# Where the large SBUF buffers of a split-float32 decoder block begin: multiples of 512 bytes, and still weights 192 bytes in

## The chip, the cores and the metric

The kernel runs on one core of a Trainium2 chip. The metric is the device time of one execution in microseconds (us). The engines are named as the profile names them: PE is TensorE's matrix multiplication, PEld its weight load, DVE is VectorE, ACT is ScalarE, POOL is GpSimd and SP is SyncE, which here issues nearly all transfers.

## The reference

One decoder layer on 256 tokens of width 1024, in float32: a normalised input goes through one wide projection into two attention branches (8 heads each) and two gates; the gated sum of both branches goes through an output projection and a normalised residual; then comes a feed-forward part with a squared ReLU. Cut to the matrix work, which is what the change touches:

```python
proj = rms_norm(x) @ w_in                       # 1024 -> q,k,v | c_q 384 | c_kv 256 + 32 | gates 2048
q = (rms_norm(c_q) @ w_uq); kv = (rms_norm(c_kv) @ w_ukv)
o_a = moba(q, k, v) @ w_branch_a                # causal softmax, 8 heads x 64
o_b = mla(q, kv) @ w_branch_b
merged = sigmoid(g_a) * o_a + sigmoid(g_b) * o_b
x = x + rms_norm(merged @ w_out)                # 1024 x 1024
x = x + rms_norm(square(relu(rms_norm(x) @ w_up)) @ w_down)   # 1024 -> 4096 -> 1024
```

## The kernel before

**Split products.** Every large factor is cut into a high and a low part (`hi`, `lo`), so that one product is three matmuls of float32r: hi by hi, hi by lo, lo by hi (`mm3`, L179 and L182). Each matmul instruction has a stationary operand, 128 columns that PEld loads into the array (512 bytes in each partition), and a moving operand of 256, 288, 384 or 512 columns that is streamed past it (1024 to 2048 bytes in each partition). In the trace the load of the next matmul's stationary operand runs while the present matmul streams.

**Which side the weights are on.** There are two kinds of product.

- `a_chunk` (L267 on), `mms` in `mix`, the first part of the up projection (`up_a`) and `product` for the down projection keep a token operand (`xt`, `mg`, `x1`, `m`) still and move the weights, 288 to 512 columns at a time.
- `b_tile` and `nope` keep the weights still and move 256 token columns: the gates (`g*`, 16 units of 24 matmuls, 384 in all, woven into attention and done after it), `uq` and `uk` (60), the branch projections `br0` to `br7` (192), and the up projection from the fifth row block on (14 pairs, 48 matmuls each, 672).

The down projection comes once for each of 16 pairs of row blocks. The pairs in `PLAIN` are 24 matmuls of 512 moving columns. Of these, pairs 0, 5 and 10 take the weights from `t_hi` and `t_lo`, 14 and 15 from `u_hi` and `u_lo`. The 11 others have seven products (21 matmuls): first three with weights from `b_hi` and `b_lo` (9 matmuls), then four from `t_hi` and `t_lo` (12). The order of PE is that of the code. From pair to pair PE alternates 48 matmuls of the up projection with 21 or 24 of the down projection.

**How weights come.** `unit` (first half) loads a raw weight block into one of 6 `raw` buffers, ACT copies it to a `whi` buffer (5), DVE writes the difference to `wlo` (5). `load` and `split` do the same in the second half with `raw_u`, `raw_d` and the pairs of buffers `u`, `t`, `b`. SP issues these transfers in the order of the code, and each waits there until the tiles that lay in its place before have been read for the last time.

**Where buffers begin.** Pools are stacks: the pools `keep`, then `att`, grow from the left, `late` and `wts` from the right; in the second half `mlp0` takes the place of `att` and `mlp1` that of `wts` and `late`. Within a pool, tiles lie in the order in which they are first made, with their sizes. In the program before, the begins are these, in bytes past a multiple of 512 in each partition (every block that a matmul reads inside a buffer lies a multiple of 512 further on, but for the 288-column blocks):

| buffers | bytes past a multiple of 512 |
|---|---|
| `xt_hi`, `xt_lo`, `x1_hi`, `x1_lo`, `t_hi`, `t_lo`, `raw_u`, `raw_d` | 320 |
| `raw`, `whi`, `wlo`, `ct`, `mg`, `u`, `b`, `m_hi`, `m_lo` | 480 |
| `o_hi`, `o_lo` | 384 |
| `kz0`, `kz1`, `qT0` / `qT1` | 128 / 320 |

The text calls *offset* the begin of the moving operand less the begin of the next stationary operand, in bytes, by the remainder over 512. Before, it is 320 - 480 = -160, that is 352, where `xt` or `x1` moves past `whi`, `wlo` or `u`; 160 where `whi` or `wlo` moves past `xt`; 352 where `t` moves past `m`; 0 where `b` or `u` moves past `m`, `whi` or `wlo` past `mg`, `t` past `x1`; and 416 (-96) where `o` moves past `whi` or `wlo`.

Of the kernel before, what the change touches and what calls it, by code (L numbers as in the profile page):

```python
# [10 lines left out]
F32 = mybir.dt.float32  # L11
F32R = mybir.dt.float32r
# [23 lines left out]
WARM_UP = 8  # L36
LAG = 2
QUOTA_A, QUOTA_B = 1900, 1900

PLAIN = (0, 5, 10, 14, 15)  # L40

# [92 lines left out]
def block_kernel(ctx: ExitStack, tc: tile.TileContext, x, xt, pos_col, g_post_in, weights, out):  # L134
    nc = tc.nc
    table, _ = _block_table()

    keep = ctx.enter_context(tc.tile_pool(name="keep", bufs=1))

    first_half, attention_part = ExitStack(), ExitStack()  # L140
    late, wts = (first_half.enter_context(tc.tile_pool(name=n, bufs=b, side="right"))
# [11 lines left out]
    def after(later, earlier):  # L153

        tc.add_manual_dep(later.ins, earlier.ins.name,
                          mybir.DependencyInfo(mybir.DependencyClass.NoSync, mybir.DependencyReason.DATA),
                          reason="order")
# [1 line left out]
    last_split = []  # L159


    def unit(key, hi=None, lo=None, behind=None):


        off, width = table[key]
        raw = wts.tile([P, UNIT], F32, name="raw", tag="raw", bufs=6)[:, :width]
        if hi is None:
            hi = wts.tile([P, UNIT], F32R, name="whi", tag="whi")[:, :width]
            lo = wts.tile([P, UNIT], F32R, name="wlo", tag="wlo")[:, :width]
        nc.sync.dma_start(raw, weights[off:off + P * width].rearrange("(p c) -> p c", c=width))  # L170
        ops = nc.scalar.activation(hi, raw, AF.Copy), nc.vector.tensor_tensor(lo, raw, hi, op=OP.subtract)  # L171
        for op, first in zip(ops, behind or ()):
            after(op, first)
        last_split[:] = ops
        return hi, lo

    def mm3(ps, a_hi, a_lo, b_hi, b_lo, first, last, a_lo_last=False):
# [22 lines left out]
    inv_freq = att.tile([P, 16], F32, name="inv_freq")  # L200
    for i in range(16):
        nc.gpsimd.memset(inv_freq[:, i:i + 1], INV_FREQ[i])
    mask = att.tile([P, 3 * P], F32, name="mask")
    nc.gpsimd.memset(mask, 0.0)
    for c in (0, 2):
        m = mask[:, c * P:(c + 1) * P]
        nc.gpsimd.affine_select(m, m, pattern=[[-1, P]], base=0, channel_multiplier=1,
                                compare_op=OP.is_ge, fill=NEG)


    stat = keep.tile([P, 128], F32, name="stat")
    used = [0]

    def stat_cols(n):
        used[0] += n
        return stat[:, used[0] - n:used[0]]
# [86 lines left out]
    ctx.enter_context(tc.manual_schedule(engines={nc.tensor.engine}))  # L303


    zeros = att.tile([P, 512], BF16, name="zeros")
    nc.vector.memset(zeros, 0.0)
    first = stat_cols(1)
    nc.scalar.activation(first, zeros[:, :1], AF.Copy)
# [30 lines left out]
    cN = att.tile([P, NT, NC], F32, name="cN", tag="t6")  # L340
    kr = att.tile([P, NT, DQ], F32, name="kr")
    nc.gpsimd.memset(kr, 0.0)
    ss_c = stat_cols(2 * NT)
    for i, n in enumerate((QLORA, KVLORA)):
        for t in range(NT):
# [103 lines left out]
    next(v_chunk)  # L449


    o_hi = att.tile([P, 2, H // 2, S], F32R, name="o_hi", tag="m2")
    o_lo = att.tile([P, 2, H // 2, S], F32R, name="o_lo", tag="m3")

# [2 lines left out]
    def attention(br, products, v_of, scale):  # L457


        ranges = ((0, P), (P, 3 * P))  # L460
        probs, pts = {}, {}

        def softmax(h, sp):
            sm = att.tile([P, 3 * P], F32, name="sm", tag="sm", bufs=3)
            st = att.tile([P, 6], F32, name="st", tag="st", bufs=4)
            pr = att.tile([P, 3 * P], F32, name="pr", tag="pr", bufs=4)
            for t, (a, b) in enumerate(ranges):
                nc.vector.tensor_tensor_reduce(sm[:, a:b], sp[t], mask[:, a:b], scale=-scale, scalar=3.0e38,
                                               op0=OP.add, op1=OP.min, accum_out=st[:, t:t + 1])
                last_exp[0] = nc.scalar.activation(pr[:, a:b], sm[:, a:b], AF.Exp, bias=st[:, t:t + 1], scale=-1.0,  # L470
                                     accum_out=st[:, 2 + t:3 + t])
            nc.vector.reciprocal(st[:, 4:6], st[:, 2:4])
            for t, (a, b) in enumerate(ranges):
                nc.vector.tensor_scalar(pr[:, a:b], pr[:, a:b], st[:, 4 + t:5 + t], None, op0=OP.mult)
            probs[h] = pr

        def turned(h):
            pp = wk_tile()
            transposes(pp, [probs[h][:, c * P:(c + 1) * P] for c in range(3)])
            pts[h] = att.tile([P, 3 * P], F32, name="pt", tag="pt", bufs=3)  # L480
            nc.scalar.copy(pts[h], pp[:, :3 * P])

        def values(hp):
            op = wk_tile()
            for j in range(2):
                h = 2 * hp + j
                o = op[j * 64:(j + 1) * 64]
                nc.tensor.matmul(o[:, 0:S], v_of(0, h), pts[h][:, 0:S], start=True, stop=False)  # L488
                nc.tensor.matmul(o[:, P:S], v_of(1, h), pts[h][:, S:S + P], start=False, stop=True)  # L489
            nc.scalar.copy(o_hi[:, br, hp], op[:, :S])  # L490
            nc.vector.tensor_tensor(o_lo[:, br, hp], op[:, :S], o_hi[:, br, hp], op=OP.subtract)

        def step(i):
            if i < H:
                for h, sp in products(i).items():
                    softmax(h, sp)
            if 0 <= i - LAG < H:
                turned(i - LAG)
            j = i - LAG - 2
            if j >= 0 and j % 2 == 0:  # L500
                values(j // 2)

        return [lambda i=i: step(i) for i in range(H + LAG + 1)]
# [31 lines left out]
    def gate_tiles():  # L535
        for m in range(KD):
            ps = acc_tile()
            for br in range(2):
                yield from b_tile(ps[:, br * S:(br + 1) * S], unit(f"g{m}_{br}"), xt_hi, xt_lo, KD)
            nc.vector.tensor_tensor(gate(m), ps.rearrange("p (b s) -> p b s", b=2),  # L540
                                    rstd_row[:, None, :].to_broadcast([P, 2, S]), op=OP.mult)
            gates_done[0] += 1
# [7 lines left out]
    def latent_work():  # L550
# [25 lines left out]
            nc.scalar.copy(dst[:, 1:4:2], psv[64:128])  # L576

        for i in range(2):
            yield from nope(unit(f"uq{i}_0"), 256, 0, range(3), qMT[0:NOPE, 4 * i:4 * i + 4])
        u = unit("uk0")  # L580
        for i in range(2):
            yield from nope(u, 512, i, (3, 4), kMT[0:NOPE, 4 * i:4 * i + 4])
        ps = [acc_tile() for _ in range(NT)]
# [34 lines left out]
    gates_up_to(1)  # L618
    left = KD - gates_done[0]
    for m in range(KD):  # L620
        u = unit(f"br{m}")
        ps = wk_tile()
        for br in range(2):
            run(b_tile(ps[:, br * S:(br + 1) * S], u, o_hi[:, br], o_lo[:, br], 4, base=4 * br))
            sig = nc.scalar.activation(gate(m)[:, br], gate(m)[:, br], AF.Sigmoid, bias=col(B_GATE, br * KD + m))
            after(sig, last_exp[0])
        pr = att.tile([P, 2 * S], F32, name="mp", tag="mp", bufs=2)
        nc.vector.tensor_tensor(pr, ps, gate(m).rearrange("p b s -> p (b s)"), op=OP.mult)
        sm = att.tile([P, S], F32, name="ms", tag=("ra", "rb")[m % 2])
        nc.vector.tensor_tensor(sm, pr[:, :S], pr[:, S:], op=OP.add)  # L630
        nc.scalar.copy(mg_hi[:, m], sm)
        nc.vector.tensor_tensor(mg_lo[:, m], sm, mg_hi[:, m], op=OP.subtract)
        gates_up_to(max(m + 2, KD - left + 1 + m))
# [10 lines left out]

        return mlp0 if tag in ("raw_u", "raw_d", "th", "tl", "m0n", "r") else mlp1[0]

    def split(src, tag, behind=(), parts=1):

        n = src.shape[-1]
        size = {"b": 3 * 512}.get(tag, PAIR)  # L650
        hi = mlp(f"{tag}h").tile([P, size], F32R, name=f"{tag}_hi", tag=f"{tag}h")[:, :n]
        lo = mlp(f"{tag}l").tile([P, size], F32R, name=f"{tag}_lo", tag=f"{tag}l")[:, :n]
        for i in range(parts):
            c = slice(i * n // parts, (i + 1) * n // parts)
            ops = nc.scalar.activation(hi[:, c], src[:, c], AF.Copy), \  # L655
                nc.vector.tensor_tensor(lo[:, c], src[:, c], hi[:, c], op=OP.subtract)  # L656
            if behind:
                for op, first in zip(ops, behind[i]):
                    after(op, first)
        return hi, lo  # L660
# [196 lines left out]
    for i in range(WARM // 2, n_pairs):  # L857
        ps = wk_tile()
        behind = {2: (turned[0, 1], turned[1, 0]), 3: (turned[1, 1],)}.get(i, ())
        w = split(load(f"up{2 * i}", "u"), "u", behind, max(len(behind), 1))  # L860
        for j in range(2):
            run(b_tile(ps[:, j * S:(j + 1) * S], w, x1_hi, x1_lo, KD, base=j * KD))
            if i == WARM // 2 and j == 0:
                for f0 in range(0, WARM, 2):
                    m0_ps = wk_tile()
                    transposes(m0_ps, [m0[:, t, k * P:(k + 1) * P] for k in (f0, f0 + 1) for t in (1, 0)])
                    square(f0 // 2, m0_ps, False)
        square(i, ps, True)
        if i >= BEHIND:
            down(i - BEHIND, (turned[1, 1],) if i == BEHIND else ())  # L870
# [69 lines left out]
```

## Time and profile before

| | us |
|---|---|
| median of 3 runs | 371.86 (371.44 to 371.88) |
| the profiled execution's own time | 371.55 |
| its span, first to last instruction | 369.8 |
| PE busy, share of the span | 359.7 (97%) |
| DVE busy | 298.0 (81%) |
| ACT busy | 248.8 (67%) |
| moved by transfers | 66.2 MB, mean 179 GB/s |

A matmul's recorded duration is modelled and overlaps that of the next one, so the duration of a single row is not its cost. The cost is the distance from one start to the next: a stretch of the trace divided by the number of matmuls that start in it. A count (x) in a stretch takes in the one or two matmuls that began before it and are still draining: one where the earlier ones are 384 or 512 columns wide, two where they have 256 or 288. [...]

### The profile page before, as it was taken

How to read it: one execution, taken by the hardware profiler on the slowest of the kernel's cores; microseconds unless marked ns; L12 is line 12 of the kernel's file. 1: busy time of each engine (PE TensorE's matmuls, PEld its weight loads, DVE VectorE, ACT ScalarE, POOL GpSimd, SP SyncE). 2: the span in 40 equal slices, each digit the busy share in tenths (PEclk: the TensorE clock that was granted, in tenths of full speed). 3: DMA queues.
4: the chain of work that ended last, by engine and by line, in shares of the span. 5: the costliest groups of instructions: out<-in, count | busy, mean ns of one | idle time of the engine just before them, and what ended most of it. 6: DMA issues, size and time to landing. Idle time of an engine off the chain costs nothing.

```text
span 369.8 us, 6081 instructions
## 1 busy us (share of the span) xinstructions
PE 359.7 (97%) x2319; PEld 321.5 (87%) x2319; DVE 298.0 (81%) x555; ACT 248.8 (67%) x375; POOL 6.5 (2%) x29
## 2 busy tenths in 40 slices
PE   8999999999999999999999999999999999999992
PEld 4699888989998999998879998889999888999881
DVE  4898898985766576796686999999989979978556
ACT  6889569996758755647289966767747766545422
POOL 6000000000000000000000000000000000000000
PEclk9999999999999999999999999999999999999997
DMA  7987763455434356574804756456564447330002
GB/s 252 403 327 244 258 205 106 125 218 152 136 96 133 113 172 178 179 268 179 334 3 165 268 194 252 180 193 228 228 217 161 170 177 284 131 115 0 2 0 113
DMA packets 15036, 66.20 MB, mean 179 GB/s; under 512 B 1696, under 2 KB 2208, under 8 KB 10912
## 3 DMA queue, kind: packets, MB, share of 16 engines
q1 hardware_dynamic: 14688, 65.30, 50.5%
q10 hardware_dynamic: 288, 0.52, 0.4%
q8 instruction: 18, 0.29, 0.3%
q14 instruction: 10, 0.08, 0.1%
q0 software_dynamic: 32, 0.00, 0.0%
HBM read 64.77 MB, written 1.05 MB: 178 GB/s over the span
## 4 chain that ended last, share of the span: by engine, by line
PE 91%; DVE 4%; DMA 2%; ACT 1%; SPq 1%; issue 1%; DVEq 0%; ACTq 0%
PE acc L182 30%; PE wk L182 27%; PE acc L179 15%; PE wk L179 13%; PE wk L368 3%; DMA raw<-in_weights 2%; PE wk L488 1%; PE wk L520 1%; ACT sq L242 1%; DVE y L898 1%; PE wk L489 1%; DVE x_lo L714 0%; PE wk L519 0%; SPq L255 0%; DVE y L685 0%
## 5 line engine op out<-in xcount | busy, mean ns | idle before, releaser
L171 DVE TENSOR_TENSOR wlo<-raw,whi 128x1024 fp32r<-128x1024 f32 (+4 forms) x58 | 65.7, 1139 | 20.3 <-ACT whi L171 20.3
L171 ACT ACTIVATE whi<-raw 128x1024 fp32r<-128x1024 f32 (+4 forms) x58 | 57.2, 992 | 28.6 <-PE acc L182 13.3
L179 PE MATMUL wk<-x_hi,u_hi 128*128 128x256 f32 x224 | 63.3, 283 | 0.0
L182 PE MATMUL wk<-x_lo,u_hi 128*128 128x256 f32 x224 | 63.3, 282 | 0.0
L182 PE MATMUL wk<-x_hi,u_lo 128*128 128x256 f32 x224 | 62.9, 281 | 0.0
L655 ACT ACTIVATE u_hi<-raw_u 128x2048 fp32r<-128x2048 f32 (+1 forms) x17 | 30.9, 1816 | 28.0 <-PE wk L182 27.9
L656 DVE TENSOR_TENSOR u_lo<-raw_u,u_hi 128x2048 fp32r<-128x2048 f32 (+1 forms) x17 | 36.8, 2162 | 10.6 <-ACT u_hi L655 10.2
L182 PEld LDWEIGHTS wk<-x_lo,u_hi 128*128 128x128 f32 x224 | 42.1, 188 | 0.6
L182 PEld LDWEIGHTS wk<-x_hi,u_lo 128*128 128x128 f32 x224 | 42.5, 190 | 0.0
L179 PEld LDWEIGHTS wk<-x_hi,u_hi 128*128 128x128 f32 x224 | 42.0, 187 | 0.6
L179 PE MATMUL acc<-xt_hi,whi 128*128 128x256 f32 x128 | 37.8, 295 | 0.0
L182 PE MATMUL acc<-xt_hi,wlo 128*128 128x256 f32 x128 | 36.1, 282 | 0.0
L182 PE MATMUL acc<-xt_lo,whi 128*128 128x256 f32 x128 | 36.0, 281 | 0.0
L656 DVE TENSOR_TENSOR t_lo<-t,t_hi 128x2048 fp32r<-128x2048 f32 x11 | 25.2, 2288 | 2.0 <-ACT t_hi L655 1.9
L805 ACT ACTIVATE m_hi<-m 128x896 fp32r<-128x896 f32 (+1 forms) x16 | 14.6, 917 | 15.9 <-DVE m L801 13.6
L179 PEld LDWEIGHTS acc<-xt_hi,whi 128*128 128x128 f32 x128 | 24.0, 188 | 1.1 <-issue 1.0
L182 PEld LDWEIGHTS acc<-xt_lo,whi 128*128 128x128 f32 x128 | 24.2, 189 | 0.1
L182 PEld LDWEIGHTS acc<-xt_hi,wlo 128*128 128x128 f32 x128 | 24.1, 188 | 0.0
L655 ACT ACTIVATE t_hi<-t 128x2048 fp32r<-128x2048 f32 x11 | 21.0, 1911 | 1.8 <-PE acc L182 1.1
L656 DVE TENSOR_TENSOR b_lo<-raw_d,b_hi 128x1536 fp32r<-128x1536 f32 x11 | 19.2, 1749 | 0.0
L806 DVE TENSOR_TENSOR m_lo<-m,m_hi 128x896 fp32r<-128x896 f32 (+1 forms) x16 | 16.6, 1044 | 2.5 <-ACT m_hi L805 2.5
L182 PE MATMUL acc<-t_lo,m_hi 128*128 128x512 f32 x46 | 18.3, 398 | 0.0
(254 smaller groups left out, 927.9 us busy)
## 6 DMA issues: line engine op xcount, KB each, us to landing
raw<-in_weights SPq DMA_DIRECT2D x44, 512.0 KB, 3.6
raw_u<-in_weights SPq DMA_DIRECT2D x17, 1024.0 KB, 5.0
raw_d<-in_weights SPq DMA_DIRECT2D x15, 1024.0 KB, 4.9
raw<-in_weights SPq DMA_DIRECT2D x7, 384.0 KB, 6.9
raw<-in_weights SPq DMA_DIRECT2D x4, 256.0 KB, 4.5
x_sb<-in_x SPq DMA_DIRECT2D x2, 512.0 KB, 8.1
g_post<-in_g_post SPq DMA_DIRECT2D x2, 512.0 KB, 5.4
raw<-in_weights SPq DMA_DIRECT2D x2, 432.0 KB, 6.8
```

Of the source, the lines that this page charges most:

```text
L171: ops = nc.scalar.activation(hi, raw, AF.Copy), nc.vector.tensor_tensor(lo, raw, hi, op=OP.subtract)
L179: nc.tensor.matmul(ps, a_hi, b_hi, start=first, stop=False)
L182: nc.tensor.matmul(ps, a, b, start=False, stop=last and i == 1)
L242: return nc.scalar.activation(sq[:, :src.shape[-1]], src, AF.Square, scale=scale, accum_out=accum)
L368: nc.tensor.transpose(ps[:n, i * P:(i + 1) * P], b, ident)
L488: nc.tensor.matmul(o[:, 0:S], v_of(0, h), pts[h][:, 0:S], start=True, stop=False)
L489: nc.tensor.matmul(o[:, P:S], v_of(1, h), pts[h][:, S:S + P], start=False, stop=True)
L520: nc.tensor.matmul(sp[:, P:3 * P], q[:, P:2 * P], k, start=True, stop=True)
L655: ops = nc.scalar.activation(hi[:, c], src[:, c], AF.Copy), \
L656: nc.vector.tensor_tensor(lo[:, c], src[:, c], hi[:, c], op=OP.subtract)
L805: nc.scalar.activation(hi, m[:, used], AF.Copy)
L806: nc.vector.tensor_tensor(lo, m[:, used], hi, op=OP.subtract)
```

## The change

Small fillers (`edge` of 480 bytes at the right, `pad_kr` of 192, `pad_o` of 256, and `stat` 192 bytes longer) move the begin of every large buffer to a multiple of 512 bytes. The tiles of `whi`, `wlo`, `u_hi` and `u_lo` become 512 bytes longer, and where the weights in them stand still (`SKEW`: gates, `uq`, `uk`, `br`, up projection from the fifth block on) the data begins 192 bytes into the tile. To make room, the mask loses a third of its width (the single triangle is now read from its right end), `zeros` shares the tag `rb`, and `mp` shares the tag `sm` with 3 buffers in place of its own 2. Unused parameters of `unit` go.

```diff
+ROW, SKEW = 512, 192
...
+    ctx.enter_context(tc.tile_pool(name="edge", bufs=1, side="right")).tile([P, 120], F32, name="edge")
...
-    def unit(key, hi=None, lo=None, behind=None):
+    def unit(key, skew=0):
         off, width = table[key]
         raw = wts.tile([P, UNIT], F32, name="raw", tag="raw", bufs=6)[:, :width]
-        if hi is None:
-            hi = wts.tile([P, UNIT], F32R, name="whi", tag="whi")[:, :width]
-            lo = wts.tile([P, UNIT], F32R, name="wlo", tag="wlo")[:, :width]
+        hi, lo = (wts.tile([P, UNIT + ROW // 4], F32R, name=n, tag=n)[:, skew // 4:skew // 4 + width]
+                  for n in ("whi", "wlo"))
...
-    mask = att.tile([P, 3 * P], F32, name="mask")
+    mask = att.tile([P, 2 * P], F32, name="mask")
...
-    stat = keep.tile([P, 128], F32, name="stat")
+    stat = keep.tile([P, 176], F32, name="stat")
...
-    zeros = att.tile([P, 512], BF16, name="zeros")
+    zeros = att.tile([P, 512], BF16, name="zeros", tag="rb")
...
     nc.gpsimd.memset(kr, 0.0)
+    att.tile([P, 48], F32, name="pad_kr")
...
+    att.tile([P, 64], F32, name="pad_o")
     o_hi = att.tile([P, 2, H // 2, S], F32R, name="o_hi", tag="m2")
...
-                nc.vector.tensor_tensor_reduce(sm[:, a:b], sp[t], mask[:, a:b], scale=-scale, scalar=3.0e38,
+                nc.vector.tensor_tensor_reduce(sm[:, a:b], sp[t], mask[:, 2 * P - (b - a):], scale=-scale, scalar=3.0e38,
...
-                yield from b_tile(ps[:, br * S:(br + 1) * S], unit(f"g{m}_{br}"), xt_hi, xt_lo, KD)
+                yield from b_tile(ps[:, br * S:(br + 1) * S], unit(f"g{m}_{br}", SKEW), xt_hi, xt_lo, KD)
...
-            yield from nope(unit(f"uq{i}_0"), 256, 0, range(3), qMT[0:NOPE, 4 * i:4 * i + 4])
-        u = unit("uk0")
+            yield from nope(unit(f"uq{i}_0", SKEW), 256, 0, range(3), qMT[0:NOPE, 4 * i:4 * i + 4])
+        u = unit("uk0", SKEW)
...
-        u = unit(f"br{m}")
+        u = unit(f"br{m}", SKEW)
...
-        pr = att.tile([P, 2 * S], F32, name="mp", tag="mp", bufs=2)
+        pr = att.tile([P, 2 * S], F32, name="mp", tag="sm", bufs=3)
...
-    def split(src, tag, behind=(), parts=1):
+    def split(src, tag, behind=(), parts=1, skew=0):
...
-        size = {"b": 3 * 512}.get(tag, PAIR)
-        hi = mlp(f"{tag}h").tile([P, size], F32R, name=f"{tag}_hi", tag=f"{tag}h")[:, :n]
-        lo = mlp(f"{tag}l").tile([P, size], F32R, name=f"{tag}_lo", tag=f"{tag}l")[:, :n]
+        size = {"b": 3 * 512, "u": PAIR + ROW // 4}.get(tag, PAIR)
+        hi = mlp(f"{tag}h").tile([P, size], F32R, name=f"{tag}_hi", tag=f"{tag}h")[:, skew // 4:skew // 4 + n]
+        lo = mlp(f"{tag}l").tile([P, size], F32R, name=f"{tag}_lo", tag=f"{tag}l")[:, skew // 4:skew // 4 + n]
...
-        w = split(load(f"up{2 * i}", "u"), "u", behind, max(len(behind), 1))
+        w = split(load(f"up{2 * i}", "u"), "u", behind, max(len(behind), 1), SKEW)
```

With it the offset becomes 0 wherever weights move (but for some 288-column blocks) and -192, that is 320, wherever they stand still.

## Rows read from the trace of the kernel before

**Rows 1.** The page: busy time, share and instructions of each engine.
```profile
PE 359.7 (97%) x2319; PEld 321.5 (87%) x2319; DVE 298.0 (81%) x555; ACT 248.8 (67%) x375; POOL 6.5 (2%) x29
```

**Rows 2.** The page: the chain that ended last, by engine.
```profile
PE 91%; DVE 4%; DMA 2%; ACT 1%; SPq 1%; issue 1%; DVEq 0%; ACTq 0%
```

**Rows 3.** Stretches with 512 moving columns: length, each engine's busy time, clock, transfers.
```profile
163.55:184.37 20.82, 20.82 (x94) 17.27 (x93) 14.88 (x21) 10.52 (x14) 0.00 (x0) 1.00 0.65 252
33.46:44.46 11.00, 11.00 (x49) 8.85 (x48) 9.04 (x23) 7.30 (x13) 0.00 (x0) 1.00 0.78 244
211.60:217.20 5.60, 5.60 (x26) 4.51 (x25) 5.60 (x10) 5.60 (x6) 0.00 (x0) 1.00 0.81 294
222.96:227.85 4.89, 4.89 (x23) 3.96 (x22) 4.89 (x4) 4.80 (x5) 0.00 (x0) 1.00 0.35 106
```

**Rows 4.** PE's instructions in order of time, `u` past `m`, from 351.36: start, duration.
```profile
351.36 0.40 PE L179 MATMUL acc<-u_hi,m_hi 128*128 128x512 f32 x1
...
353.66 0.39 PE L182 MATMUL acc<-u_hi,m_lo 128*128 128x512 f32 x1
...
355.48 0.39 PE L179 MATMUL acc<-u_hi,m_hi 128*128 128x512 f32 x1
```

**Rows 5.** Stretches with 256 moving columns, then 384 and 288; columns as in rows 3.
```profile
217.20:222.95 5.75, 5.75 (x49) 5.74 (x48) 5.75 (x7) 1.62 (x2) 0.00 (x0) 1.00 0.54 178
135.46:141.21 5.75, 5.75 (x50) 5.75 (x49) 3.96 (x6) 2.75 (x4) 0.00 (x0) 1.00 0.60 182
149.47:163.54 14.07, 14.07 (x122) 14.07 (x121) 12.25 (x18) 8.99 (x13) 0.00 (x0) 1.00 0.67 227
126.55:129.40 2.85, 2.85 (x26) 2.85 (x25) 1.23 (x1) 1.06 (x1) 0.00 (x0) 1.00 0.46 172
63.71:65.15 1.44, 1.44 (x14) 1.44 (x13) 1.44 (x5) 1.44 (x7) 0.00 (x0) 1.00 0.00 0
18.74:27.06 8.32, 8.32 (x49) 8.31 (x48) 7.93 (x46) 7.04 (x12) 0.00 (x0) 1.00 0.86 321
27.06:33.45 6.39, 6.39 (x49) 6.39 (x49) 5.78 (x33) 6.39 (x11) 0.00 (x0) 1.00 0.78 280
```

**Rows 6.** PE's instructions in order of time, `kz` past `qT`, at 75 us.
```profile
75.33 0.28 PE L179 MATMUL wk<-kz,qT 128*128 128x256 f32 x1
75.44 0.40 PE L182 MATMUL wk<-kz,qT 128*128 128x256 f32 x2
75.68 0.39 PE L179 MATMUL wk<-kz,qT 128*128 128x512 f32 x1
```

**Rows 7.** DVE's costliest groups from 217 to 346 us: count, busy, mean ns, idle before.
```profile
L656 DVE TENSOR_TENSOR u_lo<-raw_u,u_hi 128x2048 fp32r<-128x2048 f32 x13 | 29.8, 2289 | 7.2 <-ACT u_hi L655 6.8 <-PE acc L182 0.3
L656 DVE TENSOR_TENSOR t_lo<-t,t_hi 128x2048 fp32r<-128x2048 f32 x10 | 22.9, 2289 | 2.0 <-ACT t_hi L655 1.9
```

**Rows 8.** DVE's busy time in four up-and-down rounds, with their sum.
```profile
227.86:238.51 10.65, 10.39 (x12) 1.00 0.57 212
...
281.83:292.49 10.66, 10.59 (x13) 1.00 0.57 199
303.14:313.79 10.65, 10.33 (x14) 1.00 0.75 259
sum 42.61, DVE 40.58; mean DVE 10.15
```

**Rows 9.** SP's queue in order of time, around the first loads of the second half.
```profile
158.15 0.38 SPq L665 DMA_DIRECT2D raw_u<-in_weights  x1
```

**Rows 10.** DVE's instructions in order of time from 165 to 176 us.
```profile
165.96 0.42 DVE L632 TENSOR_TENSOR mg_lo<-ms,mg_hi 128x256 fp32r<-128x256 f32 x1
...
174.13 1.22 DVE L171 TENSOR_TENSOR wlo<-raw,whi 128x1024 fp32r<-128x1024 f32 x1
```

**Rows 11.** The tile `raw_u` from 140 to 215 us: ACT's first reading of it, its transfers.
```profile
L655 ACT ACTIVATE t_hi<-raw_u x1: 1902/1902/1902, 170.0 to 170.0; 128x2048 fp32r<-128x2048 f32 x1
...
DMA to landing us min/median/max: 4.9/5.4/7.3
```

More of the change, by code (lines that the diff above doesn't have):

```diff
@@ L159, in block_kernel @@
     last_split = []
-    def unit(key, hi=None, lo=None, behind=None):
+    def unit(key, skew=0):
         off, width = table[key]
         raw = wts.tile([P, UNIT], F32, name="raw", tag="raw", bufs=6)[:, :width]
-        if hi is None:
-            hi = wts.tile([P, UNIT], F32R, name="whi", tag="whi")[:, :width]
-            lo = wts.tile([P, UNIT], F32R, name="wlo", tag="wlo")[:, :width]
+        hi, lo = (wts.tile([P, UNIT + ROW // 4], F32R, name=n, tag=n)[:, skew // 4:skew // 4 + width]
+                  for n in ("whi", "wlo"))
         nc.sync.dma_start(raw, weights[off:off + P * width].rearrange("(p c) -> p c", c=width))
[L171 to L174, printed above, removed]
+        last_split[:] = nc.scalar.activation(hi, raw, AF.Copy), nc.vector.tensor_tensor(lo, raw, hi, op=OP.subtract)
         return hi, lo
@@ L202, in block_kernel @@
         nc.gpsimd.memset(inv_freq[:, i:i + 1], INV_FREQ[i])
-    mask = att.tile([P, 3 * P], F32, name="mask")
+    mask = att.tile([P, 2 * P], F32, name="mask")
     nc.gpsimd.memset(mask, 0.0)
[L205 to L208, printed above, removed]
-    stat = keep.tile([P, 128], F32, name="stat")
+    nc.gpsimd.affine_select(mask[:, P:], mask[:, P:], pattern=[[-1, P]], base=0, channel_multiplier=1,
+                            compare_op=OP.is_ge, fill=NEG)
+    stat = keep.tile([P, 176], F32, name="stat")
     used = [0]
```

## The prediction

> **What bounds the kernel now.** I read the page first: PE is busy 97% of the span, more than any other engine [rows 1], and the chain of work that ended last is 91% PE [rows 2]. So time is saved where the next matmul starts sooner, and nearly nowhere else. As recorded durations of matmuls overlap, I then read stretches: a stretch holds one kind of product, and its length over the matmuls that start in it is the price of one. [...]
>
> With 512 moving columns: the output projection has 92 starts in 20.82 us (two of its 94 are tails), 226 ns each; the tail of the down projection, once settled, has 8 in 1.82 us, 227 ns [rows 3, 4]. Both have offset 0. The k projection (offset 160) has 47 starts in 11.00 us, 234 ns; a `PLAIN` pair (offset 352) has 24 in 5.60 us, 233 ns; another pair (`b` at 0, then `t` at 352) has 21 in 4.89 us, 233 ns [rows 3]. These are the same instruction with the same shapes, and 7 ns lie between the offsets.
>
> With 256: up projection 48 in 5.75 us, 119.8 ns (352); gates after attention the same, 119.8 (352); `uk` 12 in 1.44 us, 120.0 (0); branch projections 120 in 14.07 us, 117.3, and in a shorter stretch 24 in 2.85 us, 118.8 (416) [rows 5]. With 384: 173.3 (160). With 288: 133.1 (mixed) [rows 5].
>
> From 288 to 512 columns the price rises from 133.1 to 227, 0.42 ns a column, so 256 columns alone are 107.3 ns. What is left over the columns: about 12.5 ns for 256 at 0 and 352, for 288 and for 384 at 160, and for 512 at 0; some 19 ns for 512 at 160 and 352; 10 to 11.5 ns for 256 at 416. So a price that hangs on the offset is there, but not in one rule for all widths, and the offset that 1308 of the matmuls will get, 320, has no settled row.
>
> **Part by part.** *Moving weights to offset 0.* A run that enters this state from another one doesn't settle at once: at the end of the down projection the first ten starts take 2.30 us, 230 ns each, and only then come 227 [rows 4]. I give every down pair that start. `PLAIN` pairs 0, 5 and 10: 2.30 + 14 x 0.227 = 5.48 us in place of 5.60 [rows 3], 0.12 x 3 = 0.36. The 11 pairs with `b` and `t`: 2.30 + 11 x 0.227 = 4.80 in place of 4.89, 0.09 x 11 = 1.0. The k projection: 47 x 7 ns = 0.33. The q projection, the first on the page, waits for its data in its first half: 24 x 7 ns = 0.17. v, cut up by transposes, at 230: 48 x 4 ns = 0.19. `mg`, `up_a`, `uv`, pairs 14 and 15 and the last products have offset 0 already: 0. c_q and c_kv cost no more than the least that any offset shows: 0. Sum 2.1 us, bounds 1.0 (only settled runs gain) and 2.7 (everything at 227).
>
> *Still weights to offset 320.* The lower bound is the columns alone, 107.3 ns. The upper one adds to 119.8 the 7.3 ns that a bad offset adds at 512 columns: 127.1. Between them three rows bear on it. Nearest in bytes is 352 (119.8), 32 bytes away; the other one on that side is 416, where the still weights begin 96 bytes past the moving tokens (117.3 to 118.8). Exactly at 320 there are only single starts: in the scores, `kz` past `qT` has offsets 320, 0, 0, and its three starts take 75.68 - 75.33 = 0.35 us, 117 each [rows 6], though settled 0 takes 120. I take 117.5, which these single starts and the branch rows share. Up projection 672 x 2.3 = 1.55 us, gates 384 x 2.3 = 0.88, `uq` and `uk` 60 x 2.5 = 0.15, branches 192 x about 0. Sum 2.6 us, bounds: gain of 14.8 at 107.3 ns (672 + 384 + 60 times 12.5, 192 times 10.4, minus what other engines hold back, below), loss of 10.0 at 127.1.
>
> *Whether the others keep up.* DVE must write the lo parts in the same time. In an up-and-down round of 10.65 us it is idle 0.51 us on the mean of four [rows 8]. The forecast takes 48 x 2.3 ns + 0.09 = 0.20 us out of a round, so DVE still hides; were the 256s to fall to 111 ns (0.42 + 0.09), its idle time would be used up and it would pace PE. The splits that the new offsets touch cost the same whatever the offset: `u_lo` reads 320 and 480, `t_lo` 480 and 320, both 2289 ns [rows 7]. So DVE and ACT: 0.
>
> *The filler, the shared tags and one transfer.* With `zeros` taking the tag `rb`, that slot now lies among the first tiles of `att`, inside the place of the first `raw_u` buffer. The last reader of `rb` is the eighth `mg_lo`, which ends at 166.38 us [rows 10]; the load of `raw_u` went out at 158.15 [rows 9]. Held until 166.4, it lands 5.4 us later (at most 7.3), at 171.8 to 173.7, and ACT's first reading moves from 170.0 by 1.8 to 3.7 us [rows 11]. Behind that reading, in order on ACT and DVE, stands the split of the last `out` block, whose lo part ends at 174.13 + 1.22 = 175.35 [rows 10]. PE wants it at its 60th matmul of the stage, 163.55 + 59 x 0.2263 = 176.9 [rows 3]. So 1.55 us cover it, and 0.25 to 2.1 us would not be covered. The loads behind it on SP's queue are used much later. I take 0.2 us, as the median landing says. If that cover were gone altogether the price would be 1.8. The smaller mask, `mp` in three slots, `zeros` in a slot that is next written long after the warm-up, and the fillers add no instruction and no wait: 0.
>
> Total: 2.1 + 2.6 - 0.2 = 4.5 us. The profiled execution took 371.55 us (span 369.8 and what lies around it), 0.31 below the median of the runs; 371.55 - 4.5 = 367.05, and from the median 367.4. I predict 367.4.
>
> **The rivals.**
>
> A. *At 256 columns 320 is like 352.* For it: 352 and 0 both settle at 120, and 352 is the nearest row in bytes. Then the branches rise from 117.7 to 119.8: 192 x 2.1 = 0.4 lost, 2.1 gained, 0.2 lost at the load: 371.86 - 1.5 = 370.4.
>
> B. *At 256 columns 320 is a bad offset, and slower.* The place is the up projection and the gates, the price up to 127.1 ns, as 512 columns pay 7 ns at two of three offsets. It decides from where 1116 x (p - 119.8) + 192 x (p - 117.7) passes 1.9 us: p = 120.9. At 123.5, midway to the bound, it is 4.1 + 1.1 - 1.9 = 3.3 us slower: 375.2. Against it: no row of 256, 288 or 384 columns pays more than 12.5 to 13 ns over its columns [rows 5].
>
> C. *The begin of a buffer does nothing;* the 7 ns come from something else that differs between the stages, such as which engines write SBUF beside PE. Then 371.9. Against it: `PLAIN` pairs and the tail read the same `m`, with the same shapes, and differ in where their weights lie [rows 3, 4]. [...]
>
> D. *320 is better than any offset seen.* At 114 ns: 1116 x 5.8 + 192 x 3.7 = 7.2 us, with the 1.9 above 9.1: 362.8. Below 111 DVE paces PE in the rounds.
>
> **How the numbers follow.** The forecast (256 columns at 116 to 119 ns, 365.4 to 369.4 us): 0.42. A (up to 120.5): 0.22. D: 0.15. B: 0.13. C: 0.08. The range of 8 in 10 reaches from 362.5, which leaves out the better half of D, to 372.0, which takes in A and C and leaves out nearly all of B. A measurement of this kernel tells 0.2%, 0.7 us, from no change. Faster: forecast, A and D, less 0.02 where A and the held load together come within 0.7 us: 0.77. Same: C, those 0.02 and the edge of B: 0.11. Slower: the rest of B, 0.12.
>
> **What would show it.** In the profile after: stretches of the k projection and of `t` past `m` at 227 ns a start, if the first part is right; the up projection's 48 starts in 5.64 us (5.75 for A, over 5.8 for B, 5.5 for D); branches unchanged near 117.5; the first `raw_u` load after the last `mg_lo`, and no wait of PE over 0.3 us near 177 us; PE still on 90% of the chain. Wrong it would be if 320 is not at all like 416, which no row settles, if the scheduler puts DVE's work in another order, or if a held transfer reaches PE.

## The result and the profile after

The median is 366.83 us in four runs (366.47 to 367.28), against 371.81 for the kernel before beside it: a ratio of 0.9868, 95% interval 0.9851 to 0.9886, faster by 1.3%. The forecast was 367.4. The profiled execution took 366.97 us with a span of 365.2; before it was 371.55 and 369.8, so 4.6 us are to be found in the trace.

The page of the kernel after, its first part and the chain that ended last [rows 1, 2]:

```profile
PE 354.0 (97%) x2319; PEld 318.1 (87%) x2319; DVE 297.6 (81%) x555; ACT 248.7 (68%) x375; POOL 6.1 (2%) x28
...
PE 90%; DVE 4%; DMA 2%; ACT 1%; SPq 1%; issue 1%; DVEq 0%; ACTq 0%
```

PE runs the same 2319 matmuls, has become shorter by 5.7 us of busy time, and still ends the chain. What shrank is seen in the stretches. Each line is a stretch from its first start to the first start of what follows: length, busy time (count) of PE, PE's weight loads, DVE, ACT and POOL, the clock granted to TensorE as a share of the full one, the transfers. First those of 512 columns: the output projection, the k projection, `PLAIN` pairs 0 and 5, and a pair with `b` and `t` [rows 3].

```profile
162.28:183.10 20.82, 20.82 (x94) 17.22 (x93) 14.76 (x20) 10.62 (x14) 0.00 (x0) 1.00 0.77 300
33.60:44.51 10.91, 10.91 (x50) 8.97 (x49) 9.14 (x24) 7.57 (x14) 0.00 (x0) 1.00 0.76 237
210.15:215.66 5.51, 5.51 (x26) 4.52 (x25) 5.51 (x10) 5.51 (x5) 0.00 (x0) 1.00 0.85 308
262.99:268.44 5.45, 5.45 (x26) 4.51 (x25) 5.42 (x5) 3.04 (x3) 0.00 (x0) 1.00 0.49 204
221.31:226.08 4.77, 4.77 (x23) 3.95 (x22) 4.77 (x5) 4.55 (x4) 0.00 (x0) 1.00 0.30 88
```

The output projection, at offset 0 before and after, is unchanged at 20.82 us. The k projection has 48 starts in 10.91 us, 227.3 ns (234 before); the down projection's pairs have 24 in 5.51 or 5.45 (5.60 before) and 21 in 4.77 (4.90 before, from first start to first start), 227 to 230 ns.

Then stretches of 256 columns: the up projection, gates after attention, the last 120 starts of the branch projections, 24 of their earlier starts [rows 5], and one whole up-and-down round [rows 8].

```profile
215.66:221.31 5.65, 5.65 (x49) 5.64 (x48) 5.65 (x6) 1.92 (x3) 0.00 (x0) 1.00 0.47 165
134.37:140.02 5.65, 5.65 (x50) 5.65 (x49) 3.97 (x6) 2.75 (x4) 0.00 (x0) 1.00 0.60 186
148.15:162.27 14.12, 14.12 (x122) 14.12 (x121) 12.27 (x18) 8.99 (x13) 0.00 (x0) 1.00 0.54 156
125.53:128.36 2.83, 2.83 (x26) 2.83 (x25) 1.22 (x1) 1.06 (x1) 0.00 (x0) 1.00 0.52 179
226.08:236.50 10.42, 10.42 (x70) 9.59 (x69) 10.42 (x13) 7.31 (x7) 0.00 (x0) 1.00 0.57 208
```

Up projection and gates: 48 starts in 5.65 us, 117.7 ns, in place of 119.8. The 120 branch starts in 14.12 us make 117.7, where it was 117.3; the shorter stretch has 24 in 2.83, 117.9, where it was 118.8. A round takes 10.42 us, 0.23 less. The clock column reads 1.00 in every stretch, as in the stretches before, so the clock explains none of these differences.

Where the 4.6 us lie, from the first starts of the stages in the two traces: from the start to k, 0.14 lost (33.46 before, 33.60 after); from k to the output projection 1.41 gained (163.55 - 33.46 = 130.09, then 162.28 - 33.60 = 128.68); from there to the second half of the first up group nothing (202.89 - 163.55 = 39.34, then 201.60 - 162.28 = 39.32); from there to the last 24 matmuls of the down projection, which have 256 columns, 3.29 gained (359.56 - 202.89 = 156.67, then 354.98 - 201.60 = 153.38). In this last part are ten up-and-down rounds of 10.65 that became 10.42 (2.3), a pair with `b` and `t` that has no up group before it (0.13) and three rounds with `PLAIN` pairs (0.26 each); the last products of 512 columns add 0.04. Together 4.6.

### The profile page after: what moved, and what is told of

The parts are those of the page before. It is cut to its first block, busy times and chain, and to the rows that moved or that the text cites. A ratio compares the mean times of both kernels' runs of the same rounds, so it can differ in the third digit from the quotient of the medians.

```text
span 365.2 us, 6079 instructions
## 1 busy us (share of the span) xinstructions
PE 354.0 (97%) x2319; PEld 318.1 (87%) x2319; DVE 297.6 (81%) x555; ACT 248.7 (68%) x375; POOL 6.1 (2%) x28
## 4 chain that ended last, share of the span: by engine, by line
PE 90%; DVE 4%; DMA 2%; ACT 1%; SPq 1%; issue 1%; DVEq 0%; ACTq 0%
PE acc L181 29%; PE wk L181 27%; PE acc L178 15%; PE wk L178 13%; PE wk L366 3%; DMA raw<-in_weights 2%; PE wk L487 1%; PE wk L519 1%; ACT sq L239 1%; DVE y L897 1%; PE wk L488 1%; DVE x_lo L713 0%; PE wk L518 0%; SPq L252 0%; DVE y L684 0%
## 5 line engine op out<-in xcount | busy, mean ns | idle before, releaser
L181 PE MATMUL wk<-x_lo,u_hi 128*128 128x256 f32 x224 | 62.5, 279 | 0.0
L654 ACT ACTIVATE b_hi<-raw_d 128x1536 fp32r<-128x1536 f32 x11 | 16.3, 1484 | 3.6 <-DMA raw_d<-in_weights 3.6
```

The costliest lines, as they stand in the source:

```text
L181: nc.tensor.matmul(ps, a, b, start=False, stop=last and i == 1)
```

## The experiments

Where a ratio is given, the kernel was timed beside the kernel before; the sweeps are single profiled executions, read for their prices. A "settled" price is the mean distance from one start to the next once a group has left its first starts behind.

**The fillers alone, and the skew alone.** The change has two parts; each is left out once. First `SKEW` to 0, so that the offset becomes 0 where weights stand still, too.

```diff
-ROW, SKEW = 512, 192
+ROW, SKEW = 512, 0
```

> The changed kernel with all begins at multiples of 512 bytes, but the still weights at 0 too in place of 192: for their matmuls the offset becomes 0. If only the offset between the moving operand and the next still one counts, the 1308 matmuls of 256 columns go from 117.8 ns a start back to 120.0 and cost 2.2 ns each, 2.8 us more than the changed kernel's 366.8: 369.6, while the 512-column ones stay at 227. If the 192 bytes do nothing and the gain came from the alignment alone or from the shared tags: 366.8, with the up projection's 48 starts still in 5.65 us.

Measured: 369.65 us (369.14 to 369.98), ratio 0.9947 (0.9934 to 0.9959). Then the begins of before, with still weights 32 bytes into their buffers, which gives them offset 320 (but for `uq` and `uk`) and leaves moving weights at 160 and 352.

```diff
-ROW, SKEW = 512, 192
+ROW, SKEW = 512, 32
-    ctx.enter_context(tc.tile_pool(name="edge", bufs=1, side="right")).tile([P, 120], F32, name="edge")
-    stat = keep.tile([P, 176], F32, name="stat")
+    stat = keep.tile([P, 128], F32, name="stat")
```

> The changed kernel with begins 320 bytes past a multiple of 512 at the left and 480 at the right, as before the change, and the still weights 32 bytes in: offset 320 for 256 columns but for uq and uk, 160 and 352 again where 512 columns move. If the offset counts: 256 columns at 117.8 ns a start, 512 columns at 234, so the part of the gain that the moving weights gave (about 2.4 us) is lost: 369.2. If what counts is that begins are multiples of 512 and the still weights 192 in: nothing is left of the gain, 371.8, with 256 columns at 120.

Measured: 367.07 us (366.87 to 367.37), ratio 0.9882 (0.9867 to 0.9897), some 2 us less than expected. The fillers alone, an up group and the k projection:

```profile
216.91:222.66 5.75, 5.75 (x49) 5.74 (x48) 5.75 (x7) 1.76 (x2) 0.00 (x0) 1.00 0.52 177
33.28:44.19 10.91, 10.91 (x51) 8.97 (x50) 9.12 (x23) 7.57 (x14) 0.00 (x0) 1.00 0.76 236
```

The skew alone: two up groups, the products of `PLAIN` pair 5 (24 starts), the `t` products of another pair (12), the k projection (48):

```profile
226.24:231.68 5.44, 5.44 (x49) 5.43 (x48) 5.44 (x8) 2.43 (x3) 0.00 (x0) 1.00 0.81 325
268.32:273.97 5.65, 5.65 (x49) 5.65 (x48) 4.46 (x7) 2.76 (x2) 0.00 (x0) 1.00 0.82 296
262.71:268.32 5.61, 5.61 (x27) 4.51 (x26) 5.58 (x5) 3.03 (x3) 0.00 (x0) 1.00 0.52 216
233.77:236.58 2.81, 2.81 (x13) 2.26 (x12) 2.81 (x3) 2.81 (x4) 0.00 (x0) 1.00 0.56 131
33.28:44.53 11.25, 11.25 (x51) 9.00 (x50) 9.08 (x23) 7.55 (x13) 0.00 (x0) 1.00 0.79 247
```

With the fillers, k is at 227.3 ns and the up group at 119.8: the one part carries the gain at 512 columns and no other; the branches, now at offset 0, even lose 0.4 us (22.59 us before, 23.04 here, summed from first start to first start). With the skew alone, 512 columns stay at 234 as expected, and 256 columns have two prices at one offset: 5.65 us and 5.44 us for the same 48 instructions, 117.8 and 113.3 ns once settled. Nine of the 14 up groups are at 113.3, 9 x 48 x 4.45 ns = 1.9 us, which is the surprise. The two parts alone gain 1.9 and 4.5 us, and 5.0 together. Most of what is missing is in the up projection: in the kernel after all 14 groups are at 117.8, so that it takes 79.2 us in all, where the skew alone has 77.4 and the kernel before 80.6.

**The begin itself, or the distance.** All large buffers 64 bytes further, offsets unchanged.

```diff
-...tile([P, 120], F32, name="edge")
+...tile([P, 104], F32, name="edge")
-    stat = keep.tile([P, 176], F32, name="stat")
+    stat = keep.tile([P, 192], F32, name="stat")
```

> The changed kernel with every large buffer 64 bytes further on, so that none begins at a multiple of 512 and every offset stays as it is. If only the offset counts: the same time, 366.8 within 0.5 us, 256 columns at 117.8 and 512 at 227. If the multiple of 512 itself counts (each matmul's operand crossing one boundary more): 512 columns at 230 or more and 368.5 to 372.

Measured: 366.71 us (366.42 to 366.89), ratio 0.9869 (0.9855 to 0.9882), the kernel after within its spread. Up groups are at 117.8, the k projection at 227.3. So a begin at a multiple of 512 bytes is worth nothing by itself; the distance between the moving and the still operand counts. As the begins of `hi` and `lo` are the same here, the run doesn't tell whether it is the still operand in use or the one that is loaded next.

**The held load.** `zeros` in a slot of its own, so that the first `raw_u` load needn't wait for the last `mg_lo`.

```diff
-    zeros = att.tile([P, 512], BF16, name="zeros", tag="rb")
+    zeros = att.tile([P, 512], BF16, name="zeros")
```

> The changed kernel with zeros in a slot of its own, so that the slot rb lies further on again and the first raw_u load of the second half no longer waits for the last mg_lo: it goes out near 157 us in place of 165. If the held load was covered (PE shows no wait near 177 us in the changed kernel): 366.8, the same. If it cost what the prediction set down for it: 0.2 us less, 366.6; if its cover was gone: up to 1.8 us less, 365.0.

Measured: 366.74 us (366.57 to 367.0), ratio 0.9871 (0.9857 to 0.9884): no difference. SP's queue, first in the kernel after, then with `zeros` apart [rows 9]:

```profile
165.19 0.33 SPq L664 DMA_DIRECT2D raw_u<-in_weights  x1
```

```profile
156.38 0.38 SPq L664 DMA_DIRECT2D raw_u<-in_weights  x1
```

The change did hold the load, by 8.8 us against this run, to 0.1 us behind the eighth `mg_lo` (164.68 + 0.42 = 165.10 us). ACT's first reading then starts at 170.0 in the kernel after:

```profile
L654 ACT ACTIVATE t_hi<-raw_u x1: 1916/1916/1916, 170.0 to 170.0; 128x2048 fp32r<-128x2048 f32 x1
...
DMA to landing us min/median/max: 4.7/4.8/8.8
```

That is 4.8 us after the issue, and PE waits for nothing between 160 and 185 us. Its four waits of the whole run, in us, times, longest:

```profile
PE wk L178 <- ACT whi L173: 1.4, 2, 0.8
PE wk L309 <- DVE stat L635: 1.3, 1, 1.3
PE acc L181 <- DVE x_lo L713: 0.9, 1, 0.9
PE wk L181 <- DVE wlo L173: 0.5, 1, 0.5
```

**A sweep of the still offset.** A single execution. The 14 up groups get skews of 0, 32, 64, 96, 128, 160, 224, 256, 288, 320, 352, 384, 416 and 448 bytes in turn; `br` gets 480.

```diff
+SWEEP = (0, 32, 64, 96, 128, 160, 224, 256, 288, 320, 352, 384, 416, 448)
-... behind, max(len(behind), 1), SKEW)
+... behind, max(len(behind), 1), SWEEP[i - 2])
-        u = unit(f"br{m}", SKEW)
+        u = unit(f"br{m}", 480)
```

> A look at many offsets in one run: in the changed kernel the 14 pairs of the up projection begin 0, 32, 64, 96, 128, 160, 224, 256, 288, 320, 352, 384, 416 and 448 bytes into their buffers (offsets 0, 480, 448, 416, 384, 352, 288, 256, 224, 192, 160, 128, 96, 64), the branch weights 480 (offset 32); the gates stay at 192. If the settled price hangs on the offset alone: 120.0 ns a start at 0 and 352, 117.3 to 118.8 at 416 as in the kernel before. The run before showed two settled prices at the one offset of 320, 117.8 and 113.3, so at some offsets two prices, or only 113.3, may show; if no other offset reaches 113.3, the lower price needs the way of entry as well. Time about 366 to 368, which says nothing by itself.

Measured: 367.59 us. Groups with skews of 64 and 320, then of 128 and 384:

```profile
215.53:221.18 5.65, 5.65 (x49) 5.65 (x48) 5.65 (x6) 1.88 (x3) 0.00 (x0) 1.00 0.51 170
289.62:295.27 5.65, 5.65 (x49) 5.65 (x48) 5.49 (x5) 2.63 (x2) 0.00 (x0) 1.00 0.76 268
236.40:242.17 5.77, 5.77 (x49) 5.77 (x48) 5.77 (x6) 2.24 (x3) 0.00 (x0) 1.00 0.75 304
310.49:316.26 5.77, 5.77 (x49) 5.76 (x48) 5.69 (x8) 3.28 (x3) 0.00 (x0) 1.00 0.73 308
```

The settled prices by skew: 0 and 256, 120.0 ns; 32 and 288, 118.3 each; 64 and 320, 117.8; 96 and 352, 117.3; 128 and 384, 120.0; 160 and 416, 120.0; 448 (like 192), 117.8; 224, 116.7. Up groups whose skews are 256 bytes apart agree within 0.1 ns: the pattern has a period of 256 bytes, not of 512. (The branches at 480, which is 224 modulo 256, took 117.8 all the same, and not 116.7.) No offset is bad at 256 columns; no settled price passes 120.0.

**A sweep of the moving offset.** A single execution. The moving weights of the first half begin at other places (q 32, k 64, v 96, cq 256, `out` 128 and 256 bytes), and the `m` operands of the `PLAIN` pairs 64 to 320 bytes into theirs.

```diff
+MOVE = {"q": 32, "cq": 256, "k": 64, "v": 96, "uv": 96}
+STILL = {0: 64, 5: 128, 10: 192, 14: 320, 15: 320}
-... for u in unit(f"{key}{k0}"))
+... for u in unit(f"{key}{k0}", MOVE.get(key, 0)))
-        us = [unit(f"out{k}") for k in range(KD)]
+        us = [unit(f"out{k}", 128 if k < 4 else 256) for k in range(KD)]
...
```

> The same for 512 moving columns: q weights 32 bytes into their buffers, k 64, v and uv 96, the output weights 128 (first half) and 256 (second half), c_q's (384 columns) 256, and the still m of the pairs 0, 5, 10, 14 and 15 at 64, 128, 192, 320 and 320 (offsets 448, 384, 320 and 192). If 0 is the one good offset: 230 to 238 ns a start everywhere else. If only some are bad, as 160 and 352 are: 227 at several of them. If an offset below 227 shows, the alignment of the moving weights is not the best one either.

Measured: 367.79 us. The k projection (offset 64, 48 starts), `out` at 128 (48) and at 256 (45), the products of pairs 5 (offset 384) and 10 (320), 24 each, and the up group right behind pair 5:

```profile
33.59:44.61 11.02, 11.02 (x51) 8.97 (x50) 9.13 (x23) 7.58 (x14) 0.00 (x0) 1.00 0.78 240
162.51:173.66 11.15, 11.15 (x50) 9.04 (x49) 6.46 (x7) 6.97 (x7) 0.00 (x0) 1.00 0.66 250
173.66:183.87 10.21, 10.21 (x46) 8.40 (x45) 8.34 (x14) 3.65 (x8) 0.00 (x0) 1.00 0.87 343
263.66:269.25 5.59, 5.59 (x27) 4.51 (x25) 5.56 (x6) 3.04 (x3) 0.00 (x0) 1.00 0.49 204
316.39:321.88 5.49, 5.49 (x26) 4.51 (x25) 5.42 (x6) 3.03 (x3) 0.00 (x0) 1.00 0.00 0
269.25:274.69 5.44, 5.44 (x50) 5.44 (x48) 4.25 (x6) 2.76 (x2) 0.00 (x0) 1.00 0.88 322
```

512 columns by offset, settled: 0 and 256, 226.7 ns each; 64 and 320, 228.9 each; 128 and 384, 232.4 and 233.3; 192 and 448, 233.3 each; 32, 233.3; 96, 234.6. The period is 256 here as well, within 1 ns, and 0 is the best. The one up group that changed, to 113.3 ns, stands behind the products at 384; itself it has the same offset as all others.

This run also tells whether the other engines are behind the 7 ns. In the last products, `u` past `m`, there are moments in which DVE, ACT and POOL do nothing and no transfer runs. Seven starts there, first in this run at offset 192, then in the kernel after at 0:

```profile
348.65:350.28 1.63, 1.63 (x8) 1.32 (x7) 0.00 (x0) 0.00 (x0) 0.00 (x0) 1.00 0.00 0
```

```profile
347.96:349.54 1.58, 1.58 (x8) 1.31 (x7) 0.00 (x0) 0.00 (x0) 0.00 (x0) 1.00 0.00 0
```

That is 233 and 226 ns a start. The difference is there with PE and its weight loads alone at work, so it needs no other engine and no transfer beside them.

**Hi and lo apart.** A single execution, 14 pairs of begins for the up weights' hi and lo parts.

```diff
-ROW, SKEW = 512, 192
+APART = ((192, 0), (192, 32), (192, 64), (192, 96), (192, 128), (192, 160), (192, 224),
+         (0, 192), (64, 192), (128, 192), (160, 192), (224, 192), (32, 160), (128, 0))
-... behind, max(len(behind), 1), SKEW)
+... behind, max(len(behind), 1), APART[i - 2])
...
```

> The up projection's 14 weight pairs in one run, with hi and lo begun at different places: (hi, lo) bytes into the buffer = (192,0) (192,32) (192,64) (192,96) (192,128) (192,160) (192,224) (0,192) (64,192) (128,192) (160,192) (224,192) (32,160) (128,0). Two thirds of the starts are followed by a load of hi and one third by a load of lo. If each start is priced by its own operand and the next load's alone, every group shows the mean of two prices already measured, weighted 2 to 1 (hi at 192 = 117.8 and lo at 0 = 120.0 gives 118.5; lo at 192 and hi at 0 gives 119.3), and no group comes under 116.5 ns. If the price is set by a rhythm over several starts, some groups differ from that mean by more than 1 ns, and one may settle at 113.3 ns. Time as after the change, within 0.4 us.

Measured: 366.35 us. The groups with (hi, lo) at (192, 64), (192, 96), (192, 160) and (64, 192):

```profile
215.39:220.84 5.45, 5.45 (x49) 5.44 (x48) 5.45 (x6) 1.92 (x3) 0.00 (x0) 1.00 0.50 155
225.63:231.18 5.55, 5.55 (x50) 5.55 (x49) 5.55 (x9) 2.81 (x3) 0.00 (x0) 1.00 0.85 344
246.31:251.96 5.65, 5.65 (x49) 5.65 (x48) 5.65 (x7) 4.08 (x4) 0.00 (x0) 1.00 0.71 286
278.29:283.75 5.46, 5.46 (x50) 5.46 (x48) 5.46 (x9) 2.88 (x2) 0.00 (x0) 1.00 0.75 260
```

The first and the last settle at 113.3 ns, the second at 115.6, the third at 117.8. Each start by its own operand and its own neighbour would have made 117.8 for the first and the last, 117.6 for the second and 118.5 for the third (two thirds of the hi price, one third of the lo price). So the price is not a sum over single starts here; it goes with the begins of hi and lo together. The two groups at 113.3 are the same pair of begins, once either way round, 128 bytes apart. The rest: (192, 0) 117.6; (192, 32) 117.8; (192, 128) 115.6; (192, 224), (0, 192), (160, 192) and (224, 192) 117.8; (128, 192) 116.7; (128, 0) 118.3; (32, 160) 118.9.

**One more start ahead of a group.** A single execution. Each up group but the first is preceded by a start of 8 to 256 columns whose product is overwritten.

```diff
+AHEAD = (0, 16, 32, 48, 64, 80, 96, 112, 128, 160, 192, 224, 256, 8)
...
+        if AHEAD[i - 2]:
+            nc.tensor.matmul(ps[:, :AHEAD[i - 2]], w[0][:, :P], x1_hi[:, 0, :AHEAD[i - 2]], start=True, stop=True)
```

> Ahead of the up projection's groups stands one more start whose product is overwritten, with 0, 16, 32, 48, 64, 80, 96, 112, 128, 160, 192, 224, 256 and 8 columns for the 14 pairs in turn; all begins are those after the change. If the two prices at offset 320 (117.8 and 113.3 ns) are two rhythms picked by how a group is entered, some of these groups settle at 113.3 ns (48 starts in 5.44 us in place of 5.65) and the others at 117.8. If the 113.3 ns of other runs comes from the offset of the 512-column products before the group, all groups stay at 117.8 ns. The added starts cost 0.5 to 2 us in all, so the time is 366.5 to 369 us.

Measured: 368.47 us. Groups behind 80 and behind 224 columns, 49 starts each:

```profile
246.95:252.71 5.76, 5.76 (x51) 5.76 (x49) 5.76 (x7) 4.13 (x3) 0.00 (x0) 1.00 0.74 238
311.11:316.87 5.76, 5.76 (x50) 5.76 (x49) 4.69 (x7) 4.25 (x3) 0.00 (x0) 1.00 0.81 334
```

All groups settle at 117.8: a start of another length ahead of the group doesn't bring the lower price, though the run that moved pair 5's products did.

**Hi and lo apart in the whole kernel.** Two runs, with begins of (192, 224) and (192, 32) wherever weights stand still.

```diff
-ROW, SKEW = 512, 192
+ROW, SKEW = 512, (192, 224)
-        hi, lo = (wts.tile([P, UNIT + ROW // 4], F32R, name=n, tag=n)[:, skew // 4:skew // 4 + width]
-                  for n in ("whi", "wlo"))
+        hi, lo = (wts.tile([P, UNIT + ROW // 4], F32R, name=n, tag=n)[:, at // 4:at // 4 + width]
+                  for n, at in zip(("whi", "wlo"), skew))
...
```

> The still hi weights begin 192 bytes and the still lo weights 224 bytes into their buffers, in every place where the change put both at 192; nothing else is altered. If the pair (192, 224) settles at 113.3 ns wherever it is used, about 1,308 starts of 256 columns come down from 117.8 ns: 1,308 x 4.45 ns = 5.8 us, so 361.0 us after 366.8, or 361 to 362.5 us with some slow first starts in the gates' chunks of 24. If the one group at 113.3 ns was picked by what stood before it, part of the groups stay at 117.8 ns and the time is 363 to 366.8 us. If VectorE binds in the MLP's rounds (idle 0.51 us a round before, 11 rounds that get 0.21 us shorter), the gain there is smaller and waits of TensorE on VectorE appear.

> The same with hi at 192 and lo at 32 bytes, the other pair that settled at 113.3 ns. 361 to 362.5 us if the pair of begins decides; as the run with (192, 224) within 0.5 us. Should this pair take longer to settle or hold in fewer places than (192, 224), it lies above that run.

Measured: 366.70 us (366.6 to 366.79), ratio 0.9869 (0.9854 to 0.9883), and 367.25 us (366.97 to 367.46), ratio 0.9883 (0.9866 to 0.9899). These expectations rest on a slip: in the run before, two groups were read under the wrong pair, and the pairs at 113.3 ns were (192, 64) and (64, 192), as told above. (192, 224) had been at 117.8 there, and is at 117.8 in every group here:

```profile
278.53:284.17 5.64, 5.64 (x49) 5.63 (x48) 5.64 (x9) 2.88 (x2) 0.00 (x0) 1.00 0.82 264
```

So the two runs bear out the sweep of pairs as it should have been read, and the kernel with (192, 64) throughout was not tried. From the rows it could give up to 1308 x 4.45 ns = 5.8 us, an estimate; an up-and-down round would go from 10.42 to 10.21 us, where DVE with 10.15 us of work [rows 8] is as long as PE.

**What stands before a group.** From the skew alone, whose groups at 113.3 ns stand behind `t` products at offset 352: first the moving weights of q, k, v, c_q and c_kv 96 bytes further, then also the `m` operands of pairs 0, 5 and 10 by 224, which puts those products at 128.

```diff
-ROW, SKEW = 512, 192
+ROW, SKEW = 512, 32
+MOVE = {"q": 96, "cq": 96, "ckv": 96, "k": 96, "v": 96}
...
-... for u in unit(f"{key}{k0}"))
+... for u in unit(f"{key}{k0}", MOVE.get(key, 0)))
...
```

> The run without the alignment (skew alone) took 367.07 us: its b products already lie at offset 0, its t products at 352, and eleven of its up groups settled at 113.3 ns. Here the moving weights of the first projections alone begin 96 bytes further, which puts q, k, v (about 136 starts of 512 columns at 234 ns) and cq, ckv at a multiple of 256; the rest is as in that run. If the offset modulo 256 bytes sets the price of 512 columns, 136 x 7 ns = 0.9 us go: 366.1 us, k proj 48 starts in 10.9 us. If what came before picks the price of 256 columns, the groups of the MLP, far behind, keep 113.3 ns since nothing near them moves; should they fall back to 117.8 ns, 11 x 0.21 us = 2.3 us come back and the time is 368.4 us.

> As the run before it, and the products of pairs 0, 5 and 10 at offset 128 modulo 256 in place of 96 (their m operands begin 224 bytes further). In the run that moved the m operands of all these pairs, the only up group at 113.3 ns stood behind a pair at offset 128 modulo 256 (384 bytes); behind the same pairs at offset 96 modulo 256 it was 117.8 ns. If the offset of the products just before a group picks its price, the groups behind pairs 0, 5 and 10 settle at 113.3 ns as well: 3 x 0.21 = 0.6 us less than the run before it, 365.5 us. If more than that decides, they stay at 117.8 ns, and the time is as in the run before it.

Measured: 366.47 us (366.4 to 366.68), ratio 0.9865 (0.9851 to 0.988), and 366.28 us (365.89 to 366.59), ratio 0.9857 (0.9841 to 0.9874). The first of the two, the k projection and an up group behind `b` and `t`:

```profile
32.95:43.86 10.91, 10.91 (x50) 8.97 (x49) 9.13 (x24) 7.57 (x14) 0.00 (x0) 1.00 0.76 241
225.78:231.23 5.45, 5.45 (x49) 5.44 (x48) 5.45 (x8) 2.43 (x3) 0.00 (x0) 1.00 0.80 326
```

The second, the products of pair 5 and the up group behind them:

```profile
262.39:267.95 5.56, 5.56 (x27) 4.52 (x25) 5.53 (x5) 3.03 (x3) 0.00 (x0) 1.00 0.52 218
267.95:273.60 5.65, 5.65 (x49) 5.65 (x48) 4.46 (x7) 2.76 (x2) 0.00 (x0) 1.00 0.87 287
```

k is at 227.3 ns with its moving weights at offset 256: the period of 256 holds again. The first run lies 0.6 us below the skew alone, where 0.9 was expected; k and v give 0.45 of it, and what q gives can't be told from the start-up, which varies (k starts at 33.28 us with the fillers alone and at 33.60 in the kernel after, with the same begins up to there). The same nine groups as before keep 113.3 ns (nine, not the eleven that the expectation counted); those behind pairs 0, 5 and 10 stay at 117.8 at offset 128 as at 352. So the offset of the products just before a group is not enough to name its price either. With hi and lo at one offset, 113.3 ns was seen behind `b` at 0 with `t` at 352, behind one `PLAIN` pair at 384, in six of the gates' groups of 15 to 18 starts with the skew alone, and in the kernel after in two of them and in the first 12 starts of `uq`; what they share stays open. Medians of 366.28, 366.47 and 366.83 have intervals that overlap; no run here is shown to beat the kernel after.

## Why the prediction held

**PE bounds, and a start's price hangs on the offset: shown.** 371.81 to 369.65 and to 367.07 with one part each, with the same instructions, and no change with all begins moved together. Rival C, that the begin does nothing (371.9), is out, and so is its reason: the 7 ns stay where no other engine and no transfer is at work (233 and 226 ns in the last products). The runs show 226.7 to 234.6 ns for one form by where the two operands lie. They show only the dependence on the distance; the place where it arises was not shown.

**Moving weights to offset 0, 2.1 us: right, with its parts a little off.** The 11 pairs with `b` and `t` gained 4.90 - 4.77 = 0.13 us each, 1.4 in all where I had 1.0: ten starts at 230 ns were too many, since in the rounds the new runs settle after two starts (in the one from 221.31 us 0.24 and 0.23 us, then 0.227). `b`, at offset 0 before and after, gained too (2.08 to 2.05 us for its nine starts). The `PLAIN` pairs gained 0.10 (pair 0) and 0.16 (pairs 5 and 10), 0.41 in place of 0.36. The k projection gained 48 x (234.3 - 227.3) ns = 0.34 in place of 0.33, v 0.15 in place of 0.19. What q gained is not to be seen: k started 0.14 us later than before, and in runs whose q, k and begins are the same it started at other times (33.28 with the fillers alone, 33.60 here), so the start-up varies by more than the 0.17 that I gave q. Without q that is 2.3.

**Still weights to offset 320, 2.6 us at 117.5 ns: right for this kernel.** Measured 117.7 to 117.8 in nearly all groups. Summed from first start to first start, the up projection gained 1.44 us against 1.55, the gates 0.92 (47.84 to 46.92) against 0.88, `uq` and `uk` 0.16 against 0.15, and the branches nothing (22.59 and 22.61): 2.5 in all. (The 12 starts that I read as `uk` are the first 12 of `uq`, by the order of the code; the sum isn't touched by it.) Rivals A (120) and B (above 120.9) didn't come: no still offset of the sweep passes 120.0. But the price was taken from the nearest rows, and the same offset also settles at 113.3, just under D's 114. The kernel after stays out of that state nearly everywhere; had it gone in with its nine groups as with the skew alone, the time would have been some 1.9 us lower, and inside the range still.

**Others keep up: right.** PE has no wait on DVE or ACT in the rounds; its four waits are in other stages. DVE fills the first round shown (10.42 of 10.42 us) without holding PE.

**The held load, 0.2 us: the mechanism right, the price 0.** The load went out at 165.19, 0.1 us behind the last reader of `rb`, as predicted, and PE didn't wait; with the slot apart the time is the same (366.74). The landing was 4.8 us rather than 5.4, and the output stage began 1.28 us earlier, which moved the release as much as the need; 1.55 us of cover were enough.

The sum by terms: 2.3 for the moving weights in place of 2.1, 2.5 for the still ones in place of 2.6, nothing for the load in place of 0.2, and 0.14 lost at the start, which no term held: some 4.6 us against 4.5 forecast. The mechanism was right and each term near, but that the sum is off by only 0.1 us is luck, as the errors of the terms cancel.

## What to carry to other kernels

When PE ends the chain (90% of it here) and the clock column reads 1.00, compare starts of one instruction form between stages: here the k projection took 234 ns a start, and 227.3 once its buffers lay elsewhere, and the fillers and the skew cost PE no instruction (2319 matmuls before and after). Sweep the distance between the moving operand and the weights beside it in one run, one value a group, for each width and for hi and lo apart: here the two widths had different best offsets, as 512 columns settled lowest at 0 (226.7 ns), where 256 columns took 120.0, against 116.7 with a skew of 224 bytes. A price seen in one group is a candidate only: the same offset held two prices here (113.3 and 117.8 ns), so it counts once the whole kernel has been timed with it.

## What the runs showed of the hardware that was not expected

- In the sweeps both widths follow the distance modulo 256 bytes, though the change aligns to 512: 512 columns at 0 and 256 settle at 226.7 ns, at 96 at 234.6; 256 columns with skews of 128 and 384 take 120.0 each.
- The 7 ns of 512 columns need PE alone: 233 ns at offset 192 and 226 at 0, with DVE, ACT and POOL at rest and no transfer.
- One offset had two lasting prices with the skew alone: 113.3 or 117.8 ns for 256 columns at 320, the same instructions and operands, kept for whole groups of 48 starts.
- With hi and lo 64 and 192 bytes into their buffers, either way round, 256 columns settled at 113.3 ns in both groups that had it; at 113.3 and at 226.7 ns a start is about 6% over an estimate of its columns alone (107.3 and 214.6 ns), which takes the 0.42 ns a column that the prediction works out from 133.1 ns at 288 columns and 227 at 512.
